# Sums of weights made by accumulating transfers, and separate PSUM banks for a layer norm, in a hybrid decoder layer

## The chip, the cores and the metric

The kernel runs on one core of one Trainium2 chip. A core has five engines that run their own queues of instructions in order: PE (TensorE, matmuls), DVE (VectorE), ACT (ScalarE), POOL (GpSimd) and SP (SyncE, which here only issues DMAs). They meet through semaphores. SBUF holds 128 partitions of working memory, PSUM eight banks of 128 x 512 fp32 into which PE accumulates. The metric is the device time of one execution in microseconds (us); lower is better.

## The reference

```python
def reference(x, ...):
    u = rms_norm(x, norm_mix_g)
    proj = u @ w_in                                   # q, k, v, glu input, two gates
    q = rms_norm(q, q_norm_g) * HEAD_DIM ** -0.5
    k = rms_norm(k, k_norm_g)
    attn = sliding_window_attention(q, k, v, attn_sinks, rel_bias) @ w_attn_o
    # conformer_conv: glu, depthwise conv of 31 taps, silu(layer_norm(.)) @ w_conv_out
    conv = conformer_conv(glu_in, w_dw, b_dw, conv_ln_g, conv_ln_b, w_conv_out)
    merged = sigmoid(gate_attn) * attn + sigmoid(gate_conv) * conv
    x = x + merged @ w_out
    hmid = square(relu(rms_norm(x, norm_mlp_g) @ w_ff1))
    return x + hmid @ w_ff2
```

512 tokens, width 1024, 16 query and 4 key heads of 64, window 128, MLP width 4096, all in fp32.

## The kernel before, in words

Every fp32 product is made from two halves: a value is split into a high part (a cast, name ending in h) and a low part (the difference, name ending in l), and three matmuls hi x hi, hi x lo, lo x hi are accumulated. The weights are loaded raw by SP, ACT casts the high part (wh_...), DVE or POOL subtracts for the low part (wl_...).

The work runs in stages on PE: the norm and the keys and values (to about 40 us); the input projection, attention and the depthwise convolution (to 313); W_attn_o, tiles ps_wo (to about 362); W_conv_out, tiles ps_wc (to 410); W_out in two column halves, ps_wo0 and ps_wo1 (to 453); then the MLP.

Up to W_conv_out the order is a list of events: `at(p, fn, ...)` puts a piece of work at position p, and the events are sorted by p and emitted. The layer norm of the convolution lies beside W_attn_o. `mean` (mu_ps), `centre`, `square` (lsq_ct) and `square_sum` (L878, into vsum) lead to `var` (var_ps, L884) and `spread` (rv_ps). Then for each of the 8 channel tiles ct: `scale` (L896, DVE), `silu_in` (L902 tz and L903 y, ACT), `silu` (L907, DVE), `silu_hi` (L910 sTh, ACT), `silu_lo` (L913 sTl, DVE). ps_wc needs all 8 tiles of sTh and sTl, one at each step of its contraction. L612 on DVE takes each ps_wo out of PSUM. From the end of attention on, all these PSUM tiles, y_ct and lsq_ct among them, come from one pool of 6 banks.

After W_conv_out the instructions are placed by the framework's scheduler, which also decides which buffer a tile takes. In W_out the second half's weights (raw_wout1_0 to _3) are loaded by SP, cast by ACT (L1054) and POOL (L1055); the first MLP weights raw_f10_0 and _1 follow in SP's queue. `residual` (L1032) adds W_out's result to x1 on DVE and squares it on ACT (fsq), `x2_norm` makes the scale and u2_t, `x2_trans` transposes u2_t on PE (tp_m) and splits it into x2Th and x2Tl.

The MLP runs in 4 parts. In each, 8 tiles of the first product (ps_f, L190 to L192) are squared into activations (aE, aO, and sums of them, aS); then the second product is made by 7 Strassen-like products of 24 matmuls each. Its weights lie in four quarters b11, b12, b21, b22; products take single quarters or sums of them: t3 = b22 - b12, t2 = t3 + b11, t4 = b21 - t2, t1 = b12 - b11. These four sums are made on DVE, in place or into a tile tq, each 128 x 2048. A cast that prepares half h of a sum for PE is named wh_t3_{part}{h}, and so on.

Of the kernel before, what the change touches and what calls it, by code (L numbers as in the profile page):

```python
# [8 lines left out]
F32 = mybir.dt.float32  # L9
# [3 lines left out]
ALU = mybir.AluOpType  # L13
AX = mybir.AxisListType
PSUM = bass.MemoryType.PSUM
DRAM = bass.MemoryType.DRAM

P = 128
S = 512
# [33 lines left out]
def tile_hybrid_block(  # L53
# [157 lines left out]

    gp = ExitStack()
    gpool = gp.enter_context(tc.tile_pool(name="gpool", bufs=1))
    p1, p2, pps = ExitStack(), ExitStack(), ExitStack()
    att = p1.enter_context(tc.tile_pool(name="att", bufs=1))
    aux = ctx.enter_context(tc.tile_pool(name="aux", bufs=2, space=PSUM))
    ps1 = pps.enter_context(tc.tile_pool(name="ps1", bufs=2, space=PSUM))
# [125 lines left out]
    def at(pos, fn, *args):  # L343
        events.append((pos, len(events), fn, args))
# [85 lines left out]
    def load(ch):  # L430
        name, w, c0 = chunks[ch]
        if name == "q1":
            raw = att.tile([P, KD, 256], F32, name=f"raw_{name}", tag="qT", bufs=2)
        else:
            raw = wp.tile([P, KD, 256], F32, name=f"raw_{name}", tag="raw", bufs=2)
        raws[ch] = raw
        for kh in range(2):
            nc.sync.dma_start(raw[:, 4 * kh:4 * kh + 4, :],
                              w[512 * kh:512 * kh + 512, c0:c0 + 256].rearrange("(k p) c -> p k c", p=P))
# [127 lines left out]
    b = 0  # L567
# [259 lines left out]
    def close_attention():  # L827
        p1.close()
        pps.close()
        pool_of["mm"] = ctx.enter_context(tc.tile_pool(name="psp", bufs=6, space=PSUM, reuse_waits="tile"))  # L830
        lnv["pool"] = p2.enter_context(tc.tile_pool(name="ln", bufs=1, reuse_waits="tile"))
        aTh["t"] = lnv["pool"].tile([P, KD, S], F32R, name="aTh")
        lnv["sTh"] = lnv["pool"].tile([P, KD, S], F32R, name="sTh")
        lnv["sTl"] = lnv["pool"].tile([P, KD, S], F32R, name="sTl")
        lnv["vsum"] = [lnv["pool"].tile([P, S], F32, name=f"vsum{i}") for i in range(2)]
# [32 lines left out]
    def square(ct):  # L868
        vs = lnv["vsum"][ct % 2]
        if ct >= 6:  # L870
            se.activation(vs, cc[ct], AF.Square)
        else:
            sq = lnv["sq", ct] = pool_of["mm"].tile([P, S], F32, name=f"lsq_{ct}", tag="mm")
            se.activation(sq, cc[ct], AF.Square)

    def square_sum(ct):
# [20 lines left out]

    def silu_in(ct):
        tz = lt(f"tz_{ct}")
        y = pool_of["mm"].tile([P, S], F32, name=f"y_{ct}", tag="mm")  # L900
        lnv["y", ct] = (tz, y)
        se.activation(tz, cc[ct], AF.Tanh, scale=lnh[:, ct, 0:1], bias=lnh[:, ct, 1:2])  # L902
        se.activation(y, cc[ct], AF.Identity, scale=wcol[:, ct, CW + 1:CW + 2], bias=wcol[:, ct, CW + 2:CW + 3])  # L903
# [21 lines left out]
    for ct in range(KD):  # L925
        p = E + 11.1 + 1.35 * ct
        at(p, scale, ct)
        at(p + 0.5, silu_in, ct)
        at(p + 1.4, silu, ct)
        at(p + 1.7, silu_hi, ct)  # L930
        at(p + 2.75, silu_lo, ct)

    def merge_tiles():
        for n in "hl":
# [5 lines left out]
    with tc.manual_schedule(engines=START_ENGINES):  # L940
# [50 lines left out]
            pass  # L991
        for _, _, fn, args in sorted(events, key=lambda e: e[:2]):
            fn(*args)
    psp = pool_of["mm"]
    mTh, mTl = mT["h"], mT["l"]
    p2.close()
    gp.close()
# [7 lines left out]
    def quarter(name, dtype=F32):  # L1005
        return ff.tile([P, 4, S], dtype, name=name, tag="quarter", bufs=4)
# [77 lines left out]

    def sub(out, a, b):
        ve.tensor_tensor(out=out, in0=a, in1=b, op=ALU.subtract)  # L1089

    def pieces_of(src, name):

        for h in range(2):
            shape, n = [P, 2, S], f"{name}{h}"
            if h == 0:
                wh = wp.tile(shape, F32R, name=f"wh_{n}", tag="wh")
                wl = wp.tile(shape, F32R, name=f"wl_{n}", tag="wl")
            else:
                wh = ff.tile(shape, F32R, name=f"wh_{n}", tag="wh2", bufs=2)
                wl = ff.tile(shape, F32R, name=f"wl_{n}", tag="wl2", bufs=2)  # L1100
            half = src[:, 2 * h:2 * h + 2, :]
            se.copy(wh, half)  # L1102
            sub(wl, half, wh.bitcast(F32))
            yield wh, wl

    PARTS, PT = 4, DFF // P // 4
    for part in range(PARTS):
# [10 lines left out]
        def ff1_evac(ps, m):  # L1118
            c, odd = m // 2, m % 2
            if not odd:  # L1120
                rows_r[c] = row4k(f"r_{part}_{c}").rearrange("p (o q) -> p o q", o=2)
            r = rows_r[c]
            se.activation(ps, ps, AF.Relu)
            se.activation(r[:, odd, :], ps, AF.Square)
            if not odd:
                hi_lo_of(aE, c, r[:, 0, 0:256])
                return
            hi_lo_of(aO, c, r[:, 1, :])
            a11, a21, a12, a22 = r[:, 0, 0:256], r[:, 0, 256:S], r[:, 1, 0:256], r[:, 1, 256:S]
            ss_t = row4k(f"ss_{part}_{c}").rearrange("p (i q) -> p i q", i=4)  # L1130
            s3, s1, s2, s4 = (ss_t[:, i, :] for i in range(4))
            sub(s3, a11, a21)
            ve.tensor_tensor(out=s1, in0=a21, in1=a22, op=ALU.add)
            sub(s2, s1, a11)
            sub(s4, a12, s2)
            hi_lo_of(aS, c, ss_t)

        early = []
# [17 lines left out]
        def load(odd, half):  # L1156
            b = quarter(f"b{odd}{half}_{part}")
            for h in range(2):
                nc.sync.dma_start(b[:, 2 * h:2 * h + 2, :], w2[odd][:, 2 * h:2 * h + 2, half * S:half * S + S])
            return b  # L1160

        def a_of(src, i, t):
            cols = slice(t * P, t * P + P)
            if i is None:
                return lambda c: (src[0][:, c, cols], src[1][:, c, cols])
            return lambda c: (src[0][:, c, i, cols], src[1][:, c, i, cols])

        def product(a, pieces, banks, first, last, by_token=False):
            order = [(h, t) for h in range(2) for t in range(2)]
            if by_token:  # L1170
                pieces, order = list(pieces), [(h, t) for t in range(2) for h in range(2)]
            got, it = [], iter(pieces)
            for h, t in order:
                while len(got) <= h:
                    got.append(next(it))
                wh, wl = got[h]
                for j in range(2):
                    ah, al = a(t)(2 * h + j)
                    pe.matmul(banks[t], ah, wh[:, j, :], start=(first and h + j == 0), stop=False,  # L1179
                              skip_group_check=True)  # L1180
                    pe.matmul(banks[t], ah, wl[:, j, :], start=False, stop=False, skip_group_check=True)  # L1181
                    pe.matmul(banks[t], al, wh[:, j, :], start=False, stop=(last and h + j == 2),  # L1182
                              skip_group_check=True)

        def add(row, half, banks, store):
            cols = slice(half * S, half * S + S)
            for t in range(2):
                n = 2 * row + t
                ve.tensor_tensor(out=x1[n][:, cols], in0=x1[n][:, cols], in1=banks[t], op=ALU.add)
                if store and part == PARTS - 1:  # L1190
                    nc.sync.dma_start(out[n * P:(n + 1) * P, cols], x1[n][:, cols])

        def two_banks(name):
            return [psp.tile([P, S], F32, name=f"ps_{name}{t}_{part}", tag="mm") for t in range(2)]

        def S_(i):
            return lambda t: a_of(aS, i, t)

        b11, b12, b22 = load(0, 0), load(0, 1), load(1, 1)
        X, Y = two_banks("x"), two_banks("y")  # L1200
        product(lambda t: a_of(aE, None, t), pieces_of(b11, f"b11_{part}"), X, True, True)
        add(0, 0, X, False)
        tq = quarter(f"t_{part}")
        sub(tq, b22, b12)
        product(S_(0), pieces_of(tq, f"t3_{part}"), Y, True, True)
        add(1, 1, Y, False)
        ve.tensor_tensor(out=tq, in0=tq, in1=b11, op=ALU.add)
        product(S_(2), pieces_of(tq, f"t2_{part}"), X, False, True)
        add(1, 0, X, False)
        sub(b12, b12, b11)  # L1210
        b21 = load(1, 0)
        sub(tq, b21, tq)
        product(lambda t: a_of((aO[0][:, :, 256:S], aO[1][:, :, 256:S]), None, t),
                pieces_of(tq, f"t4_{part}"), Y, False, True)
        add(1, 0, Y, True)
        product(S_(1), pieces_of(b12, f"t1_{part}"), X, False, True)
        add(1, 1, X, True)
        Z = two_banks("z")
        product(lambda t: a_of(aO, None, t), pieces_of(b21, f"b21_{part}"), Z, True, True)
        add(0, 0, Z, True)  # L1220
        product(S_(3), pieces_of(b22, f"b22_{part}"), X, False, True, part == PARTS - 1)
        add(0, 1, X, True)

# [37 lines left out]
```

## Time and profile before

| | us |
|---|---|
| three runs | 793.58, 789.66, 791.65 (median 791.65) |
| the profiled run | 791.01 |
| its span | 789.1 |
| mean granted clock of TensorE | 0.998 |
| 79.56 MB moved by DMA | mean 101 GB/s |
| POOL busy | 254.4, none of it after W_out |

A row of the timeline gives the start and the length in us, the engine, the line, the operation, the tile written and the tiles read; in brackets stands how long the engine was idle before it and what ended that. "x3" after a row means three instructions in a stretch. A row by window gives, after the window and its length, the busy time of PE, PE's weight loads, DVE, ACT and POOL with the number of instructions, then the granted clock (1.00 is full), the share of the DMA engines and GB/s. The DMA rows give how many loads, how large, and the median time from issue to landing.

### The profile page before, as it was taken

Reading aid. Unit: us, or ns where it says so; the run is one execution under the profiler, and the core shown is the slowest. Engines: PE = TensorE matmul, PEld = TensorE weight load, DVE = VectorE, ACT = ScalarE, POOL = GpSimd, SP = SyncE. Lnnn points to the kernel's source line nnn. Section 1 sums busy time; section 2 is a strip of 40 time slices with the busy share of each in tenths; the row PEclk is TensorE's granted clock in tenths of the full one; section 3 lists DMA queues with packets and bytes.
Section 4 is the critical chain, followed back from the end, with each engine's and each line's share of the span. In section 5 each row is a group of like instructions: output and inputs, shape, how many; then the busy total and the mean of one; then the engine's idle time right before and its main releaser. Section 6 shows DMA issues by size and latency. Waiting matters only on the chain.

```text
span 789.1 us, 10436 instructions
## 1 busy us (share of the span) xinstructions
PE 775.8 (98%) x3960; PEld 658.2 (83%) x3960; DVE 562.3 (71%) x949; ACT 404.8 (51%) x683; POOL 254.4 (32%) x189
## 2 busy tenths in 40 slices
PE   8999999999999999998999999999999999999998
PEld 7989988898888888786888898888888888888886
DVE  5467978998888878966330886886678756875683
ACT  6445467676576655446233346443554365435640
POOL 4444978958565665423445000000000000000000
PEclk9999999999999999999999999999999999999999
DMA  7441041214141133422335344143224233331102
GB/s 255 139 154 54 3 158 54 92 43 134 53 135 54 56 105 102 166 69 91 107 107 155 100 149 157 54 159 103 68 97 148 69 105 108 107 106 54 36 19 106
DMA packets 64807, 79.56 MB, mean 101 GB/s; under 512 B 2980, under 2 KB 52180, under 8 KB 64758
## 3 DMA queue, kind: packets, MB, share of 16 engines
q1 hardware_dynamic: 64758, 78.91, 30.0%
q8 instruction: 31, 0.51, 0.3%
q14 instruction: 18, 0.15, 0.1%
HBM read 76.78 MB, written 2.12 MB: 100 GB/s over the span
## 4 chain that ended last, share of the span: by engine, by line
PE 89%; ACT 4%; DVE 3%; POOL 2%; DMA 1%; issue 1%; SPq 0%; DVEq 0%; ACTq 0%; POOLq 0%
PE ps_f L191 7%; PE ps_f L192 7%; PE ps_f L190 7%; PE ps_x L1181 4%; PE ps_x L1182 4%; PE ps_x L1179 4%; PE ps_ta L484 2%; PE ps_ta L486 2%; PE ps_g L484 2%; PE ps_ta L485 2%; PE ps_wo L198 2%; PE ps_wo L197 2%; PE ps_y L1181 2%; PE ps_y L1182 2%; PE ps_y L1179 2%; PE ps_wo L196 2%
## 5 line engine op out<-in xcount | busy, mean ns | idle before, releaser
L782 DVE SCALAR_TENSOR_TENSOR cv<-h,wcol,cv 128x512 f32<-128x512 f32 x208 | 147.5, 747 | 0.5
L191 PE MATMUL ps_f<-x2Tl,wh_f 128*128 128x512 f32 (+1 forms) x280 | 104.1, 372 | 0.1
L190 PE MATMUL ps_f<-x2Th,wh_f 128*128 128x512 f32 (+1 forms) x280 | 103.6, 371 | 0.2 <-ACT x2Th L208 0.2
L192 PE MATMUL ps_f<-x2Th,wl_f 128*128 128x512 f32 (+1 forms) x280 | 103.8, 371 | 0.0
L157 DVE TENSOR_TENSOR wl_f<-raw_f,wh_f 128x1024 fp32r<-128x1024 f32 x32 | 39.2, 1224 | 59.8 <-ACT wh_f L156 58.8
L156 ACT CAST wh_f<-raw_f 128x1024 fp32r<-128x1024 f32 x32 | 33.6, 1055 | 55.4 <-PE ps_f L191 36.9
L190 PEld LDWEIGHTS ps_f<-x2Th,wh_f 128*128 128x128 f32 x280 | 52.6, 188 | 9.6 <-ACT x2Th L208 0.5
L191 PEld LDWEIGHTS ps_f<-x2Tl,wh_f 128*128 128x128 f32 x280 | 52.7, 188 | 9.3 <-DVE x2Tl L209 0.3
L192 PEld LDWEIGHTS ps_f<-x2Th,wl_f 128*128 128x128 f32 x280 | 52.7, 188 | 9.0
L1102 ACT CAST wh_b<-b 128x1024 fp32r<-128x1024 f32 x24 | 25.3, 1056 | 40.5 <-PE ps_y L1182 13.1
L1089 DVE TENSOR_TENSOR wl_b<-b,wh_b 128x1024 fp32r<-128x1024 f32 x24 | 29.3, 1223 | 22.2 <-ACT wh_b L1102 22.2
L1102 ACT CAST wh_t<-t 128x1024 fp32r<-128x1024 f32 x24 | 24.9, 1054 | 35.5 <-DVE t L1089 15.6
L691 ACT ACTIVATE s<-s,negm 128x257 f32<-128x257 f32 (+1 forms) x64 | 30.4, 478 | 16.3 <-DVE negm L683 16.3
L196 PE MATMUL ps_q<-wh_q,uTh 128*128 128x256 f32 x128 | 36.6, 286 | 0.0
L198 PE MATMUL ps_q<-wh_q,uTl 128*128 128x256 f32 x128 | 36.2, 283 | 0.0
L197 PE MATMUL ps_q<-wl_q,uTh 128*128 128x256 f32 x128 | 36.2, 283 | 0.0
L715 DVE TENSOR_TENSOR pTl<-ptp,pTh 128x512 fp32r<-128x512 f32 x28 | 19.3, 691 | 23.4 <-ACT pTh L711 23.4
L774 POOL TENSOR_TENSOR side<-side,tap 128x512 f32<-128x512 f32 x24 | 31.2, 1299 | 13.6 <-ACT tap L773 13.6
L1089 DVE TENSOR_TENSOR wl_t<-t,wh_t 128x1024 fp32r<-128x1024 f32 x24 | 29.0, 1221 | 5.9 <-ACT wh_t L1102 5.4
L700 POOL TENSOR_TENSOR s<-s,r 128x1024 f32<-128x1024 f32 (+1 forms) x16 | 26.9, 1682 | 14.7 <-DVE r L695 14.7
L683 DVE CUSTOM_DVE_ANT_0 s<-sp,bias,rb_sink 128x256 f32<-128x256 f32 (+1 forms) x64 | 26.2, 446 | 5.1 <-PE sp L676 4.9
L452 POOL TENSOR_TENSOR wl_wo<-raw_wo,wh_wo 128x1024 fp32r<-128x1024 f32 x8 | 19.6, 2462 | 29.3 <-ACT wh_wo L449 29.3
(298 smaller groups left out, 2305.2 us busy)
## 6 DMA issues: line engine op xcount, KB each, us to landing
raw_f<-in_w_ff_dram SPq DMA_DIRECT2D x32, 512.0 KB, 4.3
b<-in_w_ff_dram SPq DMA_DIRECT2D x32, 512.0 KB, 4.1
x<-in_x_dram SPq DMA_DIRECT2D x8, 512.0 KB, 4.7
raw_g<-in_w_in_dram SPq DMA_DIRECT2D x8, 512.0 KB, 4.1
raw_a<-in_w_in_dram SPq DMA_DIRECT2D x8, 512.0 KB, 3.5
raw_q<-in_w_in_dram SPq DMA_DIRECT2D x8, 512.0 KB, 4.4
raw_ta<-in_w_in_dram SPq DMA_DIRECT2D x8, 512.0 KB, 4.5
raw_tc<-in_w_in_dram SPq DMA_DIRECT2D x8, 512.0 KB, 3.6
```

What stands on the lines that cost most here:

```text
L190: pe.matmul(ps, wh[:, k, :], ah[:, k, cols], start=(k == 0), stop=False)
L191: pe.matmul(ps, wh[:, k, :], al[:, k, cols], start=False, stop=False)
L192: pe.matmul(ps, wl[:, k, :], ah[:, k, cols], start=False, stop=(k == nk - 1))
L196: pe.matmul(ps, ah, wh, start=first, stop=False)
L197: pe.matmul(ps, ah, wl, start=False, stop=False)
L198: pe.matmul(ps, al, wh, start=False, stop=last)
L782: ve.scalar_tensor_tensor(out=cps[ct], in0=src, scalar=w, in1=cps[ct], op0=ALU.mult, op1=ALU.add)
L1089: ve.tensor_tensor(out=out, in0=a, in1=b, op=ALU.subtract)
L1102: se.copy(wh, half)
L1179: pe.matmul(banks[t], ah, wh[:, j, :], start=(first and h + j == 0), stop=False, skip_group_check=True)
L1181: pe.matmul(banks[t], ah, wl[:, j, :], start=False, stop=False, skip_group_check=True)
L1182: pe.matmul(banks[t], al, wh[:, j, :], start=False, stop=(last and h + j == 2), skip_group_check=True)
```

## The change

The layer norm's PSUM tiles (lsq and y) get 3 banks of their own (tag "ln"), and the products and mu_ps the other 3 (tag "mm"); the pool of 6 opens again ahead of W_out. The sTh and sTl casts move to positions p+2.4 and p+3.0.

```
-        pool_of["mm"] = ctx.enter_context(tc.tile_pool(name="psp", bufs=6, space=PSUM, reuse_waits="tile"))
+        pool_of["mm"] = p3.enter_context(tc.tile_pool(name="ps3", bufs=3, space=PSUM, reuse_waits="tile"))
+        pool_of["mm"].tile([P, S], F32, name="first", tag="ln")
...
-            sq = lnv["sq", ct] = pool_of["mm"].tile([P, S], F32, name=f"lsq_{ct}", tag="mm")
+            sq = lnv["sq", ct] = pool_of["mm"].tile([P, S], F32, name=f"lsq_{ct}", tag="ln")
...
-        y = pool_of["mm"].tile([P, S], F32, name=f"y_{ct}", tag="mm")
+        y = pool_of["mm"].tile([P, S], F32, name=f"y_{ct}", tag="ln")
...
-        at(p + 1.7, silu_hi, ct)
-        at(p + 2.75, silu_lo, ct)
+        at(p + 2.4, silu_hi, ct)
+        at(p + 3.0, silu_lo, ct)
...
-    psp = pool_of["mm"]
+    p3.close()
+    psp = ctx.enter_context(tc.tile_pool(name="psp", bufs=6, space=PSUM, reuse_waits="tile"))
```

In the second MLP product the four DVE sums go. Instead GpSimd issues loads of a quarter (two halves each) that add to what lies in SBUF. Signs are altered to fit: the activation sums s1, s2 and s4 change sign where needed, and the results for the second column half are subtracted. The products run in the order b11, t3, t2, b21, t1, t4, b22, where before it was b11, t3, t2, t4, t1, b21, b22.

```
-            ve.tensor_tensor(out=s1, in0=a21, in1=a22, op=ALU.add)
-            sub(s2, s1, a11)
-            sub(s4, a12, s2)
+            sub(s1, a22, a21)
+            for o, p, q in ((s2, s1, a11), (s4, a12, s2)):
+                ve.scalar_tensor_tensor(out=o, in0=p, scalar=-1.0, in1=q, op0=ALU.mult, op1=ALU.subtract)
...
+        def load_add(b, odd, half):
+            for h in range(2):
+                ge.dma_start(b[:, 2 * h:2 * h + 2, :], w2[odd][:, 2 * h:2 * h + 2, half * S:half * S + S],
+                             accum_op=ALU.add)
...
-                ve.tensor_tensor(out=x1[n][:, cols], in0=x1[n][:, cols], in1=banks[t], op=ALU.add)
+                ve.tensor_tensor(out=x1[n][:, cols], in0=x1[n][:, cols], in1=banks[t],
+                                 op=ALU.subtract if half else ALU.add)
...
-        b11, b12, b22 = load(0, 0), load(0, 1), load(1, 1)
+        b11, tq = load(0, 0), load(0, 1)
+        load_add(tq, 1, 1)
         X, Y = two_banks("x"), two_banks("y")
         product(lambda t: a_of(aE, None, t), pieces_of(b11, f"b11_{part}"), X, True, True)
+        load_add(b11, 0, 1)
         add(0, 0, X, False)
-        tq = quarter(f"t_{part}")
-        sub(tq, b22, b12)
         product(S_(0), pieces_of(tq, f"t3_{part}"), Y, True, True)
+        load_add(tq, 0, 0)
         add(1, 1, Y, False)
-        ve.tensor_tensor(out=tq, in0=tq, in1=b11, op=ALU.add)
+        b21 = load(1, 0)
         product(S_(2), pieces_of(tq, f"t2_{part}"), X, False, True)
+        load_add(tq, 1, 0)
         add(1, 0, X, False)
-        sub(b12, b12, b11)
-        b21 = load(1, 0)
-        sub(tq, b21, tq)
+        Z = two_banks("z")
+        product(lambda t: a_of(aO, None, t), pieces_of(b21, f"b21_{part}"), Z, True, True)
+        add(0, 0, Z, True)
+        b22 = load(1, 1)
+        product(S_(1), pieces_of(b11, f"t1_{part}"), X, False, True)
+        add(1, 1, X, True)
...
-        product(S_(1), pieces_of(b12, f"t1_{part}"), X, False, True)
-        add(1, 1, X, True)
-        Z = two_banks("z")
-        product(lambda t: a_of(aO, None, t), pieces_of(b21, f"b21_{part}"), Z, True, True)
-        add(0, 0, Z, True)
```

DVE has 907 rows of instructions where it had 923; POOL has 213 where it had 193, the new ones being these loads.

Where instructions moved, first ACT in the layer norm. Before:

```order
L903 ACTIVATE y_0_3669<-h_0_584,wcol_158 128x512
L910 ACTIVATE sTh_3357<-y_0_3669 128x512
L902 ACTIVATE tz_1_3689<-h_1_674,eps_ln_80 128x512
L903 ACTIVATE y_1_3690<-h_1_674,wcol_158 128x512
L449 CAST wh_wo3_1_3693<-raw_wo3_3516 128x1024
L910 ACTIVATE sTh_3357<-y_1_3690 128x512
L902 ACTIVATE tz_2_3710<-h_2_940,eps_ln_80 128x512
```

ACT at the same place of the changed kernel (its lines lie one or two further down):

```order
L904 ACTIVATE y_0_3670<-h_0_584,wcol_158 128x512
L903 ACTIVATE tz_1_3689<-h_1_674,eps_ln_80 128x512
L904 ACTIVATE y_1_3690<-h_1_674,wcol_158 128x512
L449 CAST wh_wo3_1_3693<-raw_wo3_3517 128x1024
L911 ACTIVATE sTh_3358<-y_0_3670 128x512
L903 ACTIVATE tz_2_3710<-h_2_940,eps_ln_80 128x512
L904 ACTIVATE y_2_3711<-h_2_940,wcol_158 128x512
L911 ACTIVATE sTh_3358<-y_1_3690 128x512
```

The cast sTh of a tile now stands behind tz and y of the next one.

Second, POOL in W_out, which nobody edited. wl_wout0_i_j are the low parts of the first half's weights, wout1l those of the second half's. Before:

```order
L157 TENSOR_TENSOR wl_wout0_1_0_4133<-rawm_wout0_1_4129,wh_wout0_1_0_4132 128x1024
L1055 TENSOR_TENSOR wout1l_0_4250<-raw_wout1_0_4252,wout1h_0_4248 128x1024
L157 TENSOR_TENSOR wl_wout0_1_1_4137<-rawm_wout0_1_4129,wh_wout0_1_1_4136 128x1024
L1055 TENSOR_TENSOR wout1l_0_4250<-raw_wout1_1_4256,wout1h_0_4248 128x1024
L1055 TENSOR_TENSOR wout1l_1_4251<-raw_wout1_2_4260,wout1h_1_4249 128x1024
```

POOL in the changed kernel:

```order
L157 TENSOR_TENSOR wl_wout0_1_0_4138<-rawm_wout0_1_4134,wh_wout0_1_0_4137 128x1024
L1057 TENSOR_TENSOR wout1l_0_4255<-raw_wout1_0_4257,wout1h_0_4253 128x1024
L1057 TENSOR_TENSOR wout1l_0_4255<-raw_wout1_1_4261,wout1h_0_4253 128x1024
L157 TENSOR_TENSOR wl_wout0_1_1_4142<-rawm_wout0_1_4134,wh_wout0_1_1_4141 128x1024
L1057 TENSOR_TENSOR wout1l_1_4256<-raw_wout1_2_4265,wout1h_1_4254 128x1024
```

wl_wout0_1_1 and the second wout1l have changed places, on ACT their high parts too; and the load of raw_wout1_2 on SP now waits for the buffer of raw_wout1_1 instead of that of rawm_wout0_1, raw_wout1_3 the other way round. A little later on DVE, the changed kernel has both low parts of raw_f10_0 ahead of the residual adds:

```order
L157 TENSOR_TENSOR wl_f10_0_0_4499<-raw_f10_0_4495,wh_f10_0_0_4498 128x1024
L157 TENSOR_TENSOR wl_f10_0_1_4542<-raw_f10_0_4495,wh_f10_0_1_4541 128x1024
L1034 TENSOR_TENSOR x1_0_4108<-x1_0_4108,ps_wo0_0_4119 128x512
L1034 TENSOR_TENSOR x1_1_4110<-x1_1_4110,ps_wo0_1_4120 128x512
L1034 TENSOR_TENSOR x1_2_4112<-x1_2_4112,ps_wo0_2_4121 128x512
```

Before, wl_f10_0_1 stood behind all four adds.

Third, ACT at the end of the first product of the MLP's second part (named 1), before:

```order
L1102 CAST wh_t2_10_5557<-t_1_5520 128x1024
L1123 ACTIVATE ps_f11_7_5437<-ps_f11_7_5437 128x512
L1124 ACTIVATE r_1_3_5428<-ps_f11_7_5437 128x512
L1115 CAST aOh_1_5163<-r_1_3_5428 128x512
L1115 CAST aSh_1_5159<-ss_1_3_5466 128x1024
L1102 CAST wh_t2_11_5573<-t_1_5520 128x1024
```

And ACT at that place in the changed kernel, where b01_1 is the tile in which the sums are made:

```order
L1124 ACTIVATE ps_f11_7_5445<-ps_f11_7_5445 128x512
L1103 CAST wh_t2_10_5568<-b01_1_5484 128x1024
L1125 ACTIVATE r_1_3_5436<-ps_f11_7_5445 128x512
L1116 CAST aOh_1_5171<-r_1_3_5436 128x512
L1103 CAST wh_b21_10_5606<-b10_1_5565 128x1024
L1103 CAST wh_t2_11_5584<-b01_1_5484 128x1024
L1116 CAST aSh_1_5167<-ss_1_3_5474 128x1024
```

wh_t2_10, which waits for an accumulating load, now stands ahead of the last square and aOh, and two more casts of weights stand ahead of the last aSh.

More of the change, by code (lines that the diff above doesn't have):

```diff
@@ L213, in tile_hybrid_block @@
     gpool = gp.enter_context(tc.tile_pool(name="gpool", bufs=1))
-    p1, p2, pps = ExitStack(), ExitStack(), ExitStack()
+    p1, p2, p3, pps = ExitStack(), ExitStack(), ExitStack(), ExitStack()
     att = p1.enter_context(tc.tile_pool(name="att", bufs=1))
```

## The prediction

> **What bounds the kernel now.** I read the page's busy times first, then busy time by window, then what TensorE (PE) waited for.
>
> ```profile
> PE 775.8 (98%) x3960; PEld 658.2 (83%) x3960; DVE 562.3 (71%) x949; ACT 404.8 (51%) x683; POOL 254.4 (32%) x189
> ...
> 470.00:550.00 80.00, 80.00 (x374) 67.11 (x374) 60.19 (x71) 41.62 (x54) 0.00 (x0) 1.00 0.32 106
> ...
> PE ps_wc L484 <- ACT sTh L910: 2.2, 1, 2.2
> PE ps_wo L484 <- DVE vsum L878: 1.6, 1, 1.6
> ```
>
> PE is busy 775.8 of 789.1 us, so all its holes together hold 13.3 us. In the MLP (the window of 80 us shown; the second figure after it is PE, the last but two the granted clock) it has none: 80 of 80 us at full clock, with VectorE (DVE) at 60. DVE time saved there buys nothing. The change does not alter how many matmuls run, so it can win only in the two holes of the layer-norm stage, and lose wherever it delays what PE needs next.
>
> **Part 1, bank of ps_wo_3 (gain).**
>
> ```profile
> 324.29 1.28 DVE L612 SCALAR_TENSOR_TENSOR ta<-ta,ps_wo 128x512 f32<-128x512 f32 x2
> ...
> 334.09 1.87 DVE L878 TENSOR_TENSOR vsum<-vsum,lsq 128x512 f32<-128x512 f32 x3
> ...
> 331.83 0.50 PE L484 MATMUL ps_wo<-aTh,wh_wo 128*128 128x512 f32 x1 [1.57 <-DVE vsum L878]
> ...
> 337.40 1.84 PE L884 MATMUL var_ps<-ones,vsum 128*128 128x1 f32 x16
> ```
>
> Now ps_wo_3 waits for a bank that a layer-norm square held. With banks of its own it takes one that L612 freed by 325.57, so 1.57 us of wait go. What is late next is var_ps (L884): PE would reach it at 337.40 - 1.57 = 335.83, but the last vsum ends at 334.09 + 1.87 = 335.96 and is used about 0.1 later. Gain: 1.57 - 0.22 = **1.35 us**.
>
> **Part 2, the casts one tile later (gain).**
>
> ```profile
> 360.01 0.69 DVE L913 SCALAR_TENSOR_TENSOR sTl<-y,sTh 128x512 fp32r<-128x512 f32 x1
> ...
> 367.00 0.77 ACT L903 ACTIVATE y<-h,wcol 128x512 f32<-128x512 f32 x1
> 368.53 0.60 ACT L910 ACTIVATE sTh<-y 128x512 fp32r<-128x512 f32 x1 [0.76 <-DVE y L907]
> ...
> 364.01 0.39 PE L484 MATMUL ps_wc<-sTh,wh_wc 128*128 128x512 f32 x1
> ...
> 366.05 0.39 PE L484 MATMUL ps_wc<-sTh,wh_wc 128*128 128x512 f32 x1
> ...
> 366.57 0.39 PE L486 MATMUL ps_wc<-sTh,wl_wc 128*128 128x512 f32 x1
> 369.18 0.79 PE L484 MATMUL ps_wc<-sTh,wh_wc 128*128 128x512 f32 x1 [2.22 <-ACT sTh L910]
> ...
> 373.11 0.39 PE L484 MATMUL ps_wc<-sTh,wh_wc 128*128 128x512 f32 x1
> ...
> 368.00:370.00 2.00, 0.82 (x2) 0.38 (x2) 1.34 (x3) 1.47 (x2) 0.82 (x1) 0.80 0.11 8
> 370.00:372.00 2.00, 2.00 (x5) 1.62 (x6) 1.25 (x3) 0.06 (x1) 1.86 (x1) 0.50 0.91 311
> 372.00:374.00 2.00, 2.00 (x8) 1.58 (x8) 1.28 (x2) 1.37 (x2) 0.52 (x1) 0.84 0.58 205
> ```
>
> Per tile ScalarE (ACT) runs tz, y, waits 0.76 for DVE's silu, then sTh. After the change it works on the next tile's tz and y meanwhile, so over eight tiles 8 x 0.76 = 6.1 us of ACT waiting go; DVE, with three operations like this sTl of 0.69 per tile and a few L612, then ends its last sTl near 364, and PE wants it at about 367. The stall vanishes. Its price: from 366.57 to 373.11 PE goes on by ten matmuls, which at the usual 0.227 apart (nine from 364.01 to 366.05) take 2.27; 6.54 - 2.27 = **4.27 us**, namely 2.38 of wait and 1.89 from the lower granted clock behind it (the 0.80, 0.50, 0.84 ahead of the last two columns). The 1.57 us hole of part 1 brought no such drop.
>
> [...]
>
> **Part 3, what moves at W_out (loss).** The buffers of raw_wout1 are re-dealt: raw_wout1_2 now waits until POOL has read raw_wout1_1, and POOL does that ahead of wl_wout0_1_1.
>
> ```profile
> 421.33 4.91 POOL L1055 TENSOR_TENSOR wout1l<-raw_wout,wout1h 128x1024 fp32r<-128x1024 f32 x2 [2.30 <-ACT wout1h L1054]
> ...
> 416.52 7.60 SPq L1051 DMA_DIRECT2D raw_wout<-in_w_out_dram  x3
> 426.27 11.85 SPq L166 DMA_DIRECT2D raw_f<-in_w_ff_dram  x6
> ...
> 416.64 2.39 POOL L157 TENSOR_TENSOR wl_wout<-rawm_wout,wh_wout 128x1024 fp32r<-128x1024 f32 x1
> ...
> raw_wout<-in_w_out_dram SPq DMA_DIRECT2D x4, 512.0 KB, 3.7
> ...
> 431.33 2.01 ACT L156 CAST wh_f<-raw_f 128x1024 fp32r<-128x1024 f32 x2 [2.78 <-DMA raw_f<-in_w_ff_dram]
> ...
> 433.56 2.47 DVE L1032 TENSOR_TENSOR x<-x,ps_wo 128x512 f32<-128x512 f32 x4
> ...
> 438.52 0.68 DVE L1032 TENSOR_TENSOR x<-x,ps_wo 128x512 f32<-128x512 f32 x1
> ...
> 443.76 0.68 DVE L1032 TENSOR_TENSOR x<-x,ps_wo 128x512 f32<-128x512 f32 x1
> ...
> 454.74 0.68 DVE L1032 TENSOR_TENSOR x<-x,ps_wo 128x512 f32<-128x512 f32 x1
> 455.51 0.69 DVE L209 TENSOR_TENSOR x2Tl<-tp_m,x2Th 128x512 fp32r<-128x512 f32 x1
> ...
> 447.91 1.03 PE L206 MATMUL tp_m<-ident,u 128*128 128x128 f32 x8
> ...
> 456.25 0.39 PE L191 MATMUL ps_f<-x2Tl,wh_f 128*128 128x256 f32 x1
> ```
>
> In before's clock: raw_wout1_2 waited only for POOL's wl_wout0_1_1, done at 416.64 + 2.39 = 419.03; now it waits for POOL's read of raw_wout1_1, 421.33 to about 423.7 (the first half of the x2 row), so it is issued 4.7 us later. It lands 3.7 us after that and is cast; POOL reads it 428.6 to 431.0 (before: the second half of its x2 row, to 426.24). Only then may raw_f10_0 go: 431.05 instead of 426.27, **4.8 us late**. Its cast is at 436.1 instead of 431.33. On DVE both lo parts of raw_f10_0 now stand ahead of the four residual adds, where one did, 1.1 us more: the adds start at about 439.4 instead of 433.56. The next lo part takes one place fewer behind them, but waits for an ACT cast that follows two squares; the first second-half add then starts at about 443.7 instead of 438.52, 5.2 us late. From there add, square, rsqrt and u2 of each token tile follow without slack (438.52 to 443.76 is one tile's round of 5.24), so the shift of 5.2 lasts: the last add 459.9, and the x2Tl queued behind it about 460.7 to 461.4. PE pays in two holes: 1.15 us at the first transpose (447.91; u2_0 is done where the next tile's add starts, 443.8 + 5.2 = 449.0), and the rest at its first L191, 461.4 instead of 456.25. Together **5.15 us**. The second hole is about 4 us, longer than the 2.22 us that dropped the clock, so I add the same **1.9 us**. A cost of nothing is its lower end, if the loads have slack that I do not see; both the late wl_wout0_1_1 (POOL done by 426.1, wanted at 426.2) and the rest are covered.
>
> **Part 4, sums by transfers (DVE to nothing, a new wait).** Sixteen DVE sums of 2.28 us go (four groups like the one shown below); PE is full there, so 0. The eight accumulating loads per part, issued by GpSimd, have no row in this trace. Three have over 10 us of slack. The tight one writes the t2 sum over t3's tile.
>
> ```profile
> L1207 DVE TENSOR_TENSOR t<-t,b x4: 2284/2284/2286, 499.3 to 744.1; 128x2048 f32<-128x2048 f32 x4
> ...
> 497.82 1.23 DVE L1089 TENSOR_TENSOR wl_t<-t,wh_t 128x1024 fp32r<-128x1024 f32 x1
> ...
> 503.13 0.58 ACT L1123 ACTIVATE ps_f<-ps_f 128x512 f32<-128x512 f32 x1
> ...
> 507.85 1.06 ACT L1102 CAST wh_t<-t 128x1024 fp32r<-128x1024 f32 x1 [0.54 <-PE ps_x L1182]
> ...
> 511.50 0.39 PE L1182 MATMUL ps_y<-wh_t,aSl 128*128 128x512 f32 x1
> ...
> raw_f<-in_w_ff_dram SPq DMA_DIRECT2D x32, 512.0 KB, 4.3
> b<-in_w_ff_dram SPq DMA_DIRECT2D x32, 512.0 KB, 4.1
> ...
> gq<-in_q_norm_g_dram SPq DMA_DIRECT2D x1, 32.0 KB, 9.6
> ```
>
> It may go out when wl_t3's first half is read (497.82 + 1.23 = 499.05) and lands L later. The cast wh_t2_10 waits for it on ACT, and queued behind are now the last Square, aOh, wh_b21_10, wh_t2_11 and aSh, the last chunk of activations; DVE likewise puts the lo parts of t2 and b21 before the rest of the sums for that chunk. wh_t2_11 cannot start before 507.85 anyway (its buffer), so aSl is done about 511.2 against 511.50. Working back on ACT (1.06 each for wh_t2_10 and wh_b21_10, 0.6 each for Square and aOh) L may be 507.85 - 3.3 - 499.05 = 5.5; DVE's queue takes some 0.3 of that, an estimate. So the chain is covered while L is below about **5.2 us**; beyond that each part stalls by L - 5.2. Bounds for L: from 4.1, the plain b loads, to 9.6, gq, the slowest landing of the page. An accumulate reads a second operand, so I take 5.9, near the plain loads but above them: 0.7 x 4 parts = **2.8 us**, in holes too short to drop the clock.
>
> [...]
>
> **Sum.** The profiled run took 791.01 (span 789.1 and 1.9 around it), 0.6 below the median of 791.65 and within the three runs. 791.0 - 1.35 - 4.27 + 5.15 + 1.9 + 2.8 = **795.2 us**.
>
> **Rivals.**
> - *Transfers as quick as plain loads.* L up to 5.2 leaves part 4 at 0: 792.4; without the clock drop at W_out 790.5. For it: the plain loads of the MLP land in 4.1 to 4.3. Against: two operands. [...]
> - *Slow accumulates, slower than before.* Place: the wait of wh_t2_10, once per part; it decides from L = 5.2. At L = 7.5 each part stalls 2.3 us, and since 2.2 us dropped the clock here, 1.9 more: 792.4 + 4 x 4.2 = 809.2. For it: several go out together.
> - *W_out has slack after all.* If raw_f10_0 comes no later in effect, only the gains stay: 791.0 - 5.6 = 785.4, with part 4 up to 788.2. For it: those loads are needed by PE only at 455.5. Against: the residual adds stand behind them on DVE.
> - *The change does not do what it says.* The layer norm still ends late (DVE, not ACT, sets it): part 2 is not gained, 799.5.
>
> **How the numbers follow.** Forecast 0.37, quick transfers 0.19, slow accumulates 0.22, slack at W_out 0.16, no gain 0.06. The range runs from 785.5 to 810: it leaves out the slow end of the accumulates. A measurement of this kernel can tell about 0.5%, 4 us, from no change: faster is below 787.7, slower above 795.6. Faster is most of the slack case, 0.15; slower is the slow accumulates, the no-gain case and four tenths of the forecast, 0.43; same the rest, 0.42.
>
> **What would show it.** Right: no PE wait at ps_wo_3 nor ps_wc_0, the clock full around 366 to 374; raw_f10_0 issued some 4.8 us later against W_out, a hole of about 4 us ahead of the first L191 with the clock at 0.5 behind it; four short PE waits on aSl or aSh in ps_y. Wrong: residual adds on time, or landings of the accumulates under 5 us or over 7.

## The result, and the profile after

| | us |
|---|---|
| before, median of four runs (789.66 to 793.98) | 792.62 |
| after, median of four runs (816.23 to 818.63) | 816.59 |
| ratio after to before, 95% interval | 1.0313 (1.0277 to 1.0349) |
| the profiled run of after; its span; mean granted clock | 816.23; 814.2; 0.985 |

The change makes the kernel 3.1% slower. The forecast of 795.2 was 21 us too low, and the time lies above its range, which ended at 810; of its cases the rival "slow accumulates" comes nearest. The page of after gives the busy times and the loads (512 KB each, the last figure is the median from issue to landing):

```profile
PE 784.8 (96%) x3960; PEld 663.0 (81%) x3960; DVE 526.3 (65%) x933; ACT 402.8 (49%) x683; POOL 293.1 (36%) x221
...
b<-in_w_ff_dram SPq DMA_DIRECT2D x32, 512.0 KB, 4.3
b<-in_w_ff_dram POOLq DMA_DIRECT2D x32, 512.0 KB, 5.9
```

DVE lost the 36 us of sums as meant; POOL's 32 more instructions are the accumulating loads. PE issues the same 3960 matmuls, yet is busy for 9.0 us more and idle for 29.4 us where it was idle for 13.3. The accumulating loads land in 5.9 us, the very value that the prediction took. The view of waits shows for what PE stood still (total, times, longest):

```profile
PE ps_y L1188 <- DVE aSl L1090: 6.6, 4, 1.7
PE ps_y L1185 <- ACT aSh L1116: 6.2, 4, 2.4
PE ps_f L191 <- DVE x2Tl L209: 3.3, 1, 3.3
...
PE ps_f L190 <- ACT wh_f L156: 1.4, 1, 1.4
PE ps_wo L196 <- DVE mTl L618: 0.8, 1, 0.8
...
PE ps_f L192 <- DVE wl_f L157: 0.7, 1, 0.7
...
PE tp_m L206 <- DVE y_m L112: 0.4, 1, 0.4
...
PE var_ps L885 <- DVE vsum L879: 0.2, 1, 0.2
```

The two layer-norm waits, ps_wc on sTh and ps_wo on vsum, are gone. Eight waits stand in the second MLP product, two in each part, and six single ones elsewhere that before did not have. By window (columns as before):

```profile
364.00:368.00 4.00, 4.00 (x19) 3.33 (x18) 1.39 (x2) 0.52 (x2) 1.46 (x1) 1.00 0.57 202
368.00:372.00 4.00, 4.00 (x20) 3.30 (x19) 1.23 (x2) 1.01 (x2) 2.40 (x1) 1.00 0.00 0
470.00:550.00 80.00, 73.85 (x335) 60.77 (x334) 47.21 (x62) 39.00 (x50) 9.22 (x8) 0.96 0.61 144
```

In W_conv_out PE and its clock are full; the MLP's 80 us, which had 80 us of PE at full clock, now hold 73.85, and 335 matmuls instead of 374.

Placing both traces side by side, from the first PE row of each stage to that of the next, gives the change by stage:

| stage | before | after | change | forecast |
|---|---|---|---|---|
| W_attn_o (layer norm beside it) | 49.10 | 47.56 | -1.54 | -1.35 |
| W_conv_out | 47.86 | 43.52 | -4.34 | -4.27 |
| W_out | 44.43 | 45.58 | +1.15 | +1.15 |
| from W_out's end to the second product of part 1 | 47.94 | 56.22 | +8.28 | +5.9 |
| t3 of the four parts | 4 x 5.44 | 11.46, 10.38, 8.63, 10.63 | +19.3 | +2.8 |
| t2 of the four parts | 4 x 5.44 | 6.52, 5.46, 5.44, 6.61 | +2.3 | 0 |

These sum to +25.2; the profiled runs differ by 816.23 - 791.01 = 25.2. The first four rows together are close to the forecast (+3.55 against +1.43). **The miss is the t3 product: 21.6 us with the t2 behind it, where 2.8 were forecast.** PE's timeline of part 1 shows the two holes in it:

```profile
517.06 0.50 PE L1185 MATMUL ps_y<-wh_t,aSh 128*128 128x512 f32 x1 [2.36 <-ACT aSh L1116]
...
519.45 0.80 PE L1188 MATMUL ps_y<-wh_t,aSl 128*128 128x512 f32 x1 [1.65 <-DVE aSl L1090]
```

PE waits for the last chunk of activations, which depends on no accumulating load. Why it is late stands on ACT and DVE:

```profile
510.74 1.05 ACT L1103 CAST wh_t<-b 128x1024 fp32r<-128x1024 f32 x1 [4.26 <-DMA b<-in_w_ff_dram]
511.69 0.59 ACT L1125 ACTIVATE r<-ps_f 128x512 f32<-128x512 f32 x1
512.32 0.62 ACT L1116 CAST aOh<-r 128x512 fp32r<-128x512 f32 x1
512.85 1.05 ACT L1103 CAST wh_b<-b 128x1024 fp32r<-128x1024 f32 x1
513.80 1.04 ACT L1103 CAST wh_t<-b 128x1024 fp32r<-128x1024 f32 x1
515.97 1.04 ACT L1116 CAST aSh<-ss 128x1024 fp32r<-128x1024 f32 x1 [1.13 <-DVE ss L1136]
```

```profile
511.82 1.22 DVE L1090 TENSOR_TENSOR wl_t<-b,wh_t 128x1024 fp32r<-128x1024 f32 x1 [7.35 <-ACT wh_t L1103]
...
514.38 1.22 DVE L1090 TENSOR_TENSOR wl_b<-b,wh_b 128x1024 fp32r<-128x1024 f32 x1
515.51 0.42 DVE L1136 SCALAR_TENSOR_TENSOR ss<-r,ss 128x256 f32<-128x256 f32 x1
515.85 1.28 DVE L1195 TENSOR_TENSOR x<-x,ps_x 128x512 f32<-128x512 f32 x2
517.04 1.22 DVE L1090 TENSOR_TENSOR wl_t<-b,wh_t 128x1024 fp32r<-128x1024 f32 x1
518.18 1.21 DVE L1090 TENSOR_TENSOR aSl<-ss,aSh 128x1024 fp32r<-128x1024 f32 x1
```

ACT stands idle for 4.26 us at the cast of t2's first half, DVE for 7.35 behind it, and both have the activations of aSh and aSl queued after weights that PE wants only one or two products later. My theory was then: **it is this order that costs the time, not the transfer.** The rival: a transfer that adds is too slow or too much serialised for its place, in whatever order it is used.

### The profile page after: what moved, and what is told of

The parts are those of the page before. It is cut to its first block, busy times and chain, and to the rows that moved or that the text cites. A ratio compares the mean times of both kernels' runs of the same rounds, so it can differ in the third digit from the quotient of the medians.

```text
span 814.2 us, 10527 instructions
## 1 busy us (share of the span) xinstructions
PE 784.8 (96%) x3960; PEld 663.0 (81%) x3960; DVE 526.3 (65%) x933; ACT 402.8 (49%) x683; POOL 293.1 (36%) x221
## 3 DMA queue, kind: packets, MB, share of 16 engines
q0 software_dynamic: 8704, 16.78, 12.8%
## 5 line engine op out<-in xcount | busy, mean ns | idle before, releaser
L1165 POOL DMA_DIRECT2D b<-in_w_ff_dram x32 | 39.1, 1222 | 313.2 <-DVE ss L1090 105.0
L191 PE MATMUL ps_f<-x2Tl,wh_f 128*128 128x512 f32 (+1 forms) x280 | 105.2, 376 | 3.3 <-DVE x2Tl L209 3.3
L1090 DVE TENSOR_TENSOR wl_t<-b,wh_t 128x1024 fp32r<-128x1024 f32 x32 | 39.1, 1222 | 51.9 <-ACT wh_t L1103 51.5
L191 PEld LDWEIGHTS ps_f<-x2Tl,wh_f 128*128 128x128 f32 x280 | 53.8, 192 | 12.5 <-DVE x2Tl L209 3.5
L1103 ACT CAST wh_t<-b 128x1024 fp32r<-128x1024 f32 x32 | 33.6, 1052 | 52.0 <-DMA b<-in_w_ff_dram 23.8
L1090 DVE TENSOR_TENSOR wl_b<-b,wh_b 128x1024 fp32r<-128x1024 f32 x24 | 29.4, 1224 | 20.6 <-ACT wh_b L1103 20.6
L715 DVE TENSOR_TENSOR pTl<-ptp,pTh 128x512 fp32r<-128x512 f32 x28 | 19.3, 690 | 23.5 <-ACT pTh L711 23.5
```

Of the source, the lines that this page charges most:

```text
L191: pe.matmul(ps, wh[:, k, :], al[:, k, cols], start=False, stop=False)
L1165: ge.dma_start(b[:, 2 * h:2 * h + 2, :], w2[odd][:, 2 * h:2 * h + 2, half * S:half * S + S], accum_op=ALU.add)
```

## The experiments

Each is timed against before, run on the same chip (medians of before 791.8 to 792.1); e6 in a single execution.

**The two halves of the change apart.** e1 is before with the own banks and the later casts (the layer-norm part of the diff); e2 is after with these undone.

> Only the layer-norm half of the change: own PSUM banks and the later casts; the second MLP product as before. Theory: the layer norm gains 5.9 us as in the changed kernel (no PE wait at ps_wo_3 or ps_wc_0), and the re-dealt buffers of raw_wout1, which come with this half alone, give most of it back (1.2 us up to the first ps_f, then a hole of about 3 us and 1.7 to 3.4 us at half clock): 790 to 792 us, ratio about 1.00. Rival, the loss lies all in the accumulating loads: 785 to 786 us.

> Only the MLP half of the change: sums by accumulating loads and the new order of products; the layer norm as before. Theory: the loss of 21 to 24 us of the four t3 products is all there without the W_out shift: 812 to 817 us, PE waiting for aSh and aSl in ps_y four times, 2.5 to 4 us each. Rival, the accumulates are late only because the layer-norm half shifts the loads ahead of them: 791 to 797 us.

| | median us | ratio to before |
|---|---|---|
| e1, layer norm alone | 794.41 | 1.0030 (1.0015 to 1.0045) |
| e2, transfers alone | 824.49 | 1.0417 (1.0392 to 1.0443) |

e1 lies above the 790 to 792 that I expected. Set beside before by the stages of the table above, its trace gains 4.3 us in W_conv_out, but nothing in W_attn_o (49.19 against 49.10), where after gained 1.5: half clock beside var_ps, which the last section shows in e5 with the same layer norm, would take that back (half of 3.41 us is 1.7, an estimate). W_out is 1.1 longer and the stage behind it 5.4, with this wait in it:

```profile
PE ps_f L191 <- DVE x2Tl L209: 3.1, 1, 3.1
```

e2 lies higher than I expected, and higher than the whole change. Its largest waits of PE:

```profile
PE ps_f L190 <- ACT wh_f L156: 8.0, 1, 8.0
PE ps_y L1186 <- DVE aSl L1088: 6.6, 4, 1.7
PE ps_y L1183 <- ACT aSh L1114: 4.6, 4, 2.0
```

The 8.0 us are new. On ACT, the cast of t3's second half in part 1 stands ahead of the casts of the next first-product weights, and it waits for the third accumulating transfer of the part. Its row in after, and its row in e2:

```profile
475.33 1.05 ACT L1103 CAST wh_t<-b 128x1024 fp32r<-128x1024 f32 x1 [10.08 <-DMA b<-in_w_ff_dram]
```

```profile
482.78 1.04 ACT L1101 CAST wh_t<-b 128x1024 fp32r<-128x1024 f32 x1 [16.69 <-DMA b<-in_w_ff_dram]
```

In after PE reaches these weights 5.6 us later, counted from W_out's end, since it has just lost the time at x2Tl; so only 1.4 and 0.7 us of the same hole remain. The two losses of the change overlap; mending W_out alone should bring this one out, though no run mends it alone.

**The order in W_out.** e3 is e1 with one thing put back: the preparation of raw_wout1_1 stands behind that of the piece which it had overtaken.

```
+        if i == 1:
+            behind(hi, made["wout0_1_1"][0])
+            behind(lo, made["wout0_1_1"][1])
```

`behind` adds an order between two instructions of one engine, without a wait.

> The layer-norm half alone, with the old order of the weight preparation at W_out put back: the two preparations of the second raw_wout1 piece are queued behind those of the last piece of the first half, on ACT and on POOL. Theory: the whole gain of the layer norm stays, 785 to 786 us, and the clock is full at the start of the MLP. Rival, the delay at W_out has another cause: 790 to 792 us as with the layer-norm half alone.

Measured: 787.35 us, 0.9947 (0.9928 to 0.9966), above the 785 to 786 expected: the half clock beside var_ps stays (mean clock 0.997 in the profiled run, as in e5, whose windows the last section shows), and so does the 1.1 us in W_out, which thus comes not from this order but from the pool that is opened again. The wait for x2Tl, 3.1 us in e1, is gone. By the medians the re-dealt order costs 794.41 - 787.35 = 7.1 us. The two traces differ by 6.5, of which 1.1 lies ahead of W_attn_o, where the code is the same; the 5.4 left are all in the stage behind W_out.

**The order behind the transfers.** e4 is after, with the casts and lows of t2 and b21 queued behind the last chunk's aSh and aSl.

```
+            if name.split("_")[0] in ('t2', 'b21'):
+                behind(hi, last["h"])
+                behind(lo, last["l"])
```

> The changed kernel with one thing more: on ACT and DVE the preparation of t2 and b21 is queued behind the last chunk of the activation sums (aSh and aSl). The accumulating loads and their bytes stay as they are. Theory: the stall is one of order, since what waits for the accumulate stands ahead of what PE needs next; t2 itself is needed 5.4 us later than that. The four waits in ps_y go, with the half clock behind them: 793 to 797 us. Rival, the transfers themselves are too slow for their place: the wait moves to the first matmul of t2, 808 us or more.

Measured: 796.30 us, 1.0061 (1.0044 to 1.0079). ACT at the place shown above:

```profile
508.73 0.62 ACT L1125 CAST aOh<-r 128x512 fp32r<-128x512 f32 x1
510.59 1.05 ACT L1125 CAST aSh<-ss 128x1024 fp32r<-128x1024 f32 x1 [1.24 <-DVE ss L1145]
512.60 1.05 ACT L1109 CAST wh_t<-b 128x1024 fp32r<-128x1024 f32 x1 [0.96 <-DMA b<-in_w_ff_dram]
```

aSh now comes first, and the cast of t2 still waits for its load but holds nobody up: every t3 takes 5.44 us again and no ps_y wait is left. This order alone takes back 816.59 - 796.30 = 20.3 us with the same transfers. That decides against the rival. What remains over before is W_out (3.3 us at x2Tl, and the clock) and the hole of part 1, 1.0 and 0.7.

**All orders mended.** e5 has the orders of e3 and e4, and t3's second half in part 1 behind the weights that PE wants first.

```
+            if name == "t3_0" and h == 1:
+                behind(hi, made["f10_2_1"][0])
+                behind(lo, made["f10_2_1"][1])
```

> The changed kernel with all three places put in order: the old order of the weight preparation at W_out, the preparation of t2 and b21 behind the last activation sums, and in the first part the preparation of t3's second half behind that of the third pair of MLP weights. All accumulating loads stay. Theory: every cost of the change is one of order, and the 36 us of VectorE time that the loads save are worth nothing, so this equals the layer-norm half with the old W_out order: 786 to 788 us. Rival, the loads cost something by themselves (32 more transfers beside the others): 790 us or more; second rival, the saved VectorE time is worth something: below 785 us.

Measured: 787.77 us, 0.9949 (0.9935 to 0.9964). That is the time of e3, which has no accumulating transfers: well ordered they cost nothing that these intervals (about 1.5 us to either side) can show, and the 36 us of DVE time that they save are worth nothing. Their landing is still 5.9.

**The price of the addition.** e6 is after without `accum_op=ALU.add`; the same loads overwrite, so the additions are left out of the computation.

> The changed kernel with the same 32 loads from GpSimd, but overwriting where they added: the additions of the four weight sums are left out, so the sums are not formed. Theory: two thirds of the 5.9 us are not due to the addition: the first bytes move 1.9 us after the issue, and the next GpSimd load starts only after the one before has landed, with addition or without; landing near 4 to 5 us, PE waits in ps_y shrink by 1 to 2 us a part: 805 to 812 us. Rival, adding costs nothing and it is GpSimd's path alone: landing stays at 5.9 us and the time at 815 to 818.

Measured, in one execution: 794.42 us. The row of these loads, and the first ones on POOL's timeline:

```profile
b<-in_w_ff_dram POOLq DMA_DIRECT2D x32, 512.0 KB, 3.8
```

```profile
459.32 1.45 POOL L1165 DMA_DIRECT2D b<-in_w_ff_dram  x2 [2.63 <-DVE y_m L116]
```

I had expected 805 to 812, with one load in flight whether it adds or not. Both were wrong. A plain load from GpSimd lands in 3.8 us and two go out back to back; adding costs 2.1 us of landing (5.9 in after), and no two accumulating ones are issued closer than 5.91 us in after. Of the aSh and aSl waits 0.3 us are left, and each t3 takes 5.8 to 6.0 us. So a quicker transfer would also have hidden the order's fault: it takes both, a load of 5.9 us and the queue behind it.

**When the tight transfer goes out.** In after it is not issued as soon as t3's first half has been read. DVE's last read of it, and POOL's rows in part 1:

```profile
502.59 1.22 DVE L1090 TENSOR_TENSOR wl_t<-b,wh_t 128x1024 fp32r<-128x1024 f32 x1
...
499.01 1.21 POOL L1165 DMA_DIRECT2D b<-in_w_ff_dram  x1 [19.72 <-DVE ss L1090]
505.06 1.22 POOL L1165 DMA_DIRECT2D b<-in_w_ff_dram  x1 [4.84 <-DVE aEl L1090]
513.46 1.21 POOL L1165 DMA_DIRECT2D b<-in_w_ff_dram  x1 [7.17 <-DVE wl_t L1090]
```

Ahead of it, at 499.01, goes a load for t1, which is wanted only in the fifth product of the part. e7 puts t2's first.

```
+        behind(adds[2], adds[4])
```

> The changed kernel with two accumulating loads of each part swapped in GpSimd's queue: the one for t2's first half goes out ahead of the one for t1's first half, which it stood behind. Theory: a GpSimd load starts only when the one before has landed (none of the 31 gaps between issues is under 5.9 us), so t2's load went out 0.8 us later than its own wait allowed; now it goes that much earlier and each part's stall shrinks by 0.8 us and perhaps some half clock: 810 to 814 us. Rival, the load ahead does not hold it up: 815 to 818 us.

Measured: 814.14 us, 1.0298 (1.0255 to 1.0341). The wait for aSh falls, that for aSl stays:

```profile
PE ps_y L1192 <- DVE aSl L1094: 6.6, 4, 1.7
...
PE ps_y L1189 <- ACT aSh L1120: 1.7, 4, 0.6
```

The load goes out 0.9 us earlier against the product's start (in part 2, 2.74 ahead of it and not 1.86), and aSh is waited for 4.5 us less over four parts. aSl is behind DVE's own queue, which this leaves as it was. The interval of the time overlaps that of after, so only the waits, not the time, carry this point.

**The two layer-norm edits apart.** e8 has the later casts alone, e9 the banks alone.

> The kernel before with nothing but the casts of the layer norm one tile later, the PSUM banks shared as before. The order at W_out stays the old one in this build. Theory: the stall at ps_wc_0 was one of ACT's order and goes without the new banks; the wait at ps_wo_3 stays: 4.3 us gained, 787 to 788 us. Rival, the later casts hold their PSUM banks longer and the shared banks run short, so that a wait appears at a ps_wo or y tile: 790 us or more.

> The kernel before with nothing but the layer norm's own PSUM banks, the casts where they were. In this build the order at W_out is the changed one. Theory: the wait of 1.57 us at ps_wo_3 goes, the stall at ps_wc_0 of some 4.3 us stays, and the re-dealt W_out order and the reopened pool cost 1.2 us and a hole of 3 us with half clock behind it, as in the layer-norm half: 795 to 798 us. Rival, the loss at W_out comes with the casts: 789 to 791 us.

| | median us | ratio to before |
|---|---|---|
| e8, later casts alone | 787.03 | 0.9946 (0.9928 to 0.9963) |
| e9, own banks alone | 797.88 | 1.0075 (1.0052 to 1.0098) |

e8 keeps W_out's old order, and its only wait left past attention of over 0.3 us is the 1.6 us of ps_wo on vsum. e9 has the new order in W_out and the 3.2 us wait at x2Tl: it is the banks that move W_out, a whole stage away from where they are used. e8, two lines, is as fast as e5 and is the version to keep.

**Could the banks be worth something?** With them the first step of W_out waits 0.83 us for a bank, in e3 and e5 too: with the pool of 6 reopened, ps_wo0_3 gets the bank of the last ps_wc, which L618 reads out.

```profile
406.93 0.50 PE L196 MATMUL ps_wo<-wh_wout,mTh 128*128 128x512 f32 x1 [0.83 <-DVE mTl L618]
```

e10 is e3 with the first half's ps_wo taken from the two old groups of three, and the pool of 6 opened only behind it.

```
+    accs = [pool_of["mm"].tile([P, S], F32, name=f"ps_wo0_{t}", tag="mm" if t == 3 else "ln") for t in range(NT)]
```

> The layer-norm half with the old W_out order, and the first half of W_out taken from the layer norm's three banks and one of the products', so that its fourth tile does not wait for the bank of ps_wc_7; the pool of 6 opens after it. Theory: the 0.84 us wait at the first step of W_out goes: 786 to 787 us against 787.4, with the kernel before at 791.9. Rival, the first tile of the second half then waits for a bank that a late residual add holds: 788 us or more.

Measured: 792.55 us, 1.0012 (1.0001 to 1.0023). The 0.8 us are gone, and a longer wait is there instead, at the second half's first bank, which a residual add still reads:

```profile
PE ps_wo L203 <- DVE x L1039: 3.2, 1, 3.2
```

## Why the prediction was wrong, point by point

**Parts 1 and 2 were right in place and size**: -1.54 and -4.34 us for the -1.35 and -4.27 forecast. Two things beside them were not seen. The reopened pool costs 0.83 us at W_out; and in e5, which has the own banks too, the clock drops to half beside var_ps (last section), where after kept it; in e1 W_attn_o takes 49.19 us, no less than before. So the gain of part 1 is not there in each execution, and e3, with both parts, is no faster than e8 with part 2 alone.

**Part 3 was right in mechanism, and near in size but for one term.** From W_out's first matmul (409.83 before, 403.90 after) the rows of before and these of after give raw_f10_0 4.1 us later (4.8 forecast), the residual adds 5.45 later (5.85), the first second-half add 4.7 later (5.2):

```profile
424.42 9.69 SPq L166 DMA_DIRECT2D raw_f<-in_w_ff_dram  x6
```

```profile
433.08 2.47 DVE L1034 TENSOR_TENSOR x<-x,ps_wo 128x512 f32<-128x512 f32 x4
...
437.26 0.68 DVE L1034 TENSOR_TENSOR x<-x,ps_wo 128x512 f32<-128x512 f32 x1
```

The hole ahead of L191 is 3.3 us (about 4), and with the half clock behind it (453.12 to 459.95 in after) e1 and e3 set the cost of the order at 5.4 in their traces (4.0 + 1.9). What the forecast placed at the first transpose, 1.15 us, is not there; the +1.15 of W_out in the table is the 0.83 above and 0.3 more, stays in e3 with the old order, and agrees by chance. Of the 8.28 us in the next stage, 2.1 are the waits for wh_f and wl_f, which belong to part 4.

**Part 4 is the step that failed.** The prediction said "the chain is covered while L is below about 5.2 us; beyond that each part stalls by L - 5.2", so 0.7 x 4 = 2.8 us "in holes too short to drop the clock". L was right, though it was a guess between bounds of 4.1 and 9.6. The 5.2 and the clock were not:

- wl_t3's first half ends 1.9 us ahead of the second product (503.81 against 505.70), not 3.15 as in before, so the load may go out 1.3 us later against PE.
- The load goes out 1.25 us after that end (505.06), not at once: the one before it, issued at 499.01, lands at 504.75, and in after none of the 31 that follow another goes out less than 0.26 us after the one ahead of it has landed. e7 shows this price on aSh.
- From the start of wh_t2 to the end of aSl it takes 519.39 - 510.74 = 8.65 us. I had added up ACT's queue to 6.65 and given DVE 0.3. DVE has t2's and b21's low parts of 1.22 each ahead of the sum that aSh needs, and two residual adds and another low part ahead of aSl.
- So PE waits not once for 0.7 but twice, 4.0 us in part 1, and 12.8 over the four parts. Of the other 8.8 us of the 21.6, about 7 are half clock: in three stretches of 3.4 to 6.8 us PE is busy for 13.9 us at 0.50. The rest, some 0.5 a part, comes with the holes too, since a hole costs a little more than the wait that the view counts: part 3 keeps the clock and loses 3.19 us for 2.6 of waits.
- In e6 GpSimd's loads land in 3.8 us, the median, and t3 is still 0.4 to 0.6 longer than 5.44. So with this order the limit lies near there and not at 5.2.

I also gave the three other kinds of transfer "over 10 us of slack". For the third one of part 1 that was false (1.4 + 0.7 us in after, 8.0 in e2): I compared its landing with the product that uses it, not with what is queued behind its cast.

**The rival was right in sign, not in its reason.** "Slow accumulates" needed L = 7.5 to reach 809.2. L was 5.9, and the time was worse still. e4 and e5 show that at this L the order behind the load's cast decides. The other rivals fell: the loads were slower than plain ones, W_out had no slack, and the layer norm did end early.

## What to carry to other kernels

Where an engine's work is replaced by a slower transfer, follow the queue of every engine behind the first instruction that waits for it, up to what the bound engine needs next; here moving four casts and four low parts in each part of the MLP behind the activations was worth 20 us with the transfers unchanged. Time taken from an engine that never sets the pace (36 us of DVE) buys nothing, so such a change can only break even. A change of a buffer pool needs its effect on order read in later stages too: three banks set apart for a layer norm cost 5 to 7 us two products further on.

## What the runs showed of the hardware that was not expected

**The clock.** In the traces of before and after the half-clock stretches, but for the one in each that the end of the run cuts off, last 3.41 or 6.83 us, and those of after (from 453.12, 517.97, 606.72 and 777.39) begin at multiples of 3.413 us from one another, wherever PE's hole began. Windows laid on that grid in after, around the t3 products of parts 1 and 3:

```profile
514.56:517.97 3.41, 0.88 (x3) 0.30 (x2) 3.41 (x5) 2.28 (x3) 0.11 (x1) 1.00 0.82 111
517.97:521.39 3.42, 1.94 (x5) 1.55 (x6) 3.16 (x4) 0.00 (x0) 1.22 (x1) 0.50 0.26 47
521.39:524.80 3.41, 3.41 (x10) 2.64 (x9) 1.57 (x2) 1.04 (x1) 0.00 (x0) 0.50 0.99 153
...
688.64:692.05 3.41, 2.06 (x8) 1.05 (x6) 3.41 (x6) 2.05 (x3) 0.00 (x0) 1.00 0.87 136
692.05:695.47 3.42, 2.16 (x9) 1.80 (x10) 3.18 (x5) 0.24 (x1) 1.22 (x1) 1.00 0.12 20
```

In part 1 a window with 3.41 - 0.88 = 2.5 us of idle PE is followed by one at 0.50, and that one, itself 1.5 us idle, by another. In part 3 the edge falls between the two holes; 1.35 and 1.26 us of idle lie in windows of their own, the clock stays, and t3 takes 8.63 us, not 11.46. In part 2 the window from 603.31 holds both holes, 1.33 and 1.26 us, and the next is at 0.50. Over the windows of this grid in before and after, up to the end of PE's work, those at full clock with up to 1.54 us of idle PE kept the clock in the next, and those with 1.90, 2.02, 2.22, 2.54 and 2.58 us lost it. Windows that were themselves at half clock were followed by another with 1.27, 1.48 and 1.68 us, and by full clock with 0.40 and less. So in these two traces two short holes count together where they share a window, 1.90 of 3.41 us sufficed, and whether a hole drops the clock depends partly on where it falls.

One kind of window lost the clock with hardly any idle time: that of var_ps, sixteen matmuls of one column. In e5:

```profile
334.51:337.92 3.41, 3.20 (x24) 2.81 (x23) 1.67 (x3) 1.24 (x2) 3.20 (x2) 1.00 0.03 2
337.92:341.33 3.41, 3.41 (x10) 2.64 (x10) 2.95 (x13) 0.00 (x0) 1.33 (x1) 0.50 0.92 305
```

PE counts as busy for 3.20 of 3.41 us there, and the next window is at half clock. The reading is that narrow matmuls count for little. In before the sixteen take 1.84 us; at that length the other matmuls cover some 1.4 us of e5's window and 2.0 count as idle, an estimate. Leaving the rows of var_ps out, the other matmuls leave at most 1.40 us uncovered in a window of after that holds them (from 333.65), and 0.94 in before (from 335.09), and there the clock stays. These fall on the line found above, but no run tested it alone.

**Accumulating loads.** One of 512 KB takes 5.9 us (5.6 to 8.8 in after) where the plain load by the same engine takes 3.8 in e6, and in after POOL never issues the next less than 5.91 us later, where in e6 two plain ones went out 0.73 us apart. The pages of after and e6 give the packets of GpSimd's loads, their MB, and their time as a share of the 16 DMA engines' span:

```profile
q0 software_dynamic: 8704, 16.78, 12.8%
```

```profile
q0 software_dynamic: 4608, 16.78, 6.1%
```

For the same bytes the accumulating loads take nearly twice the packets and twice the packet time. In after the first packet starts 1.94 us after the issue, in the median, so about 3.9 of the 5.9 us lie behind it. Why the accumulating ones go one at a time stays open: the load at 505.06 had its last visible wait over at 504.48 and left 0.3 us after the landing at 504.75, and no run here separates the queue from what writes the sum.
